# Mixer steps queued behind projections, SSD decays and RG-LRU convolutions one step ahead, FFN residual added on VectorE

## The chip, the cores and the metric

One Trainium2 chip, of which the program uses one core: TensorE (PE, with its weight loads PEld), VectorE (DVE), ScalarE (ACT), GpSimd (POOL) and the queue of SyncE (SP), which issues nearly all transfers. The metric is the device time of one execution in microseconds (us), the median over runs.

## The reference

Two layers of a diffusion backbone on 256 context and 512 latent tokens of width 1024, all float32. Each layer modulates its input, multiplies it by one wide matrix, runs four bidirectional sequence mixers on the parts of the product (A: HGRN2, B: Mamba-2 SSD, C: RG-LRU, D: retention), projects back, and then does the same with a convolutional FFN.

```python
for l in range(DEPTH):
    sh1, sc1, g1, sh2, sc2, g2 = adaln(c, ada_w[l], ada_b[l])
    u = concat([h_ctx * (1 + csc1) + csh1, h_lat * (1 + sc1) + sh1])
    mix = hybrid_mixer(u, w_in[l], ...)          # A, B, C, D, then @ w_out
    h_lat = layer_norm(ALPHA * h_lat + g1 * mix[:, CTX_LEN:], ...)
    f_lat = conv_ffn(h_lat * (1 + sc2) + sh2, ...)   # (gelu(dwconv(gate)) * up) @ w_out
    h_lat = layer_norm(ALPHA * h_lat + g2 * f_lat, ...)
    # the context stream goes the same way, in layer 0 only

def hybrid_mixer(h, ...):
    # B: y = (q k^T * masked exp(b_t - b_s)) v per chunk, plus q S exp(b_t); S carried from chunk to chunk
    # C: cx = conv4(c_x); r, gi = sigmoid(cx @ wa), sigmoid(cx @ wi) per block
    #    h = scan of a = exp(-8 r softplus(-lambda)) with input sqrt(1 - a^2) * gi * cx
    return concat([out_a, out_b, out_c, out_d]) @ w_out
```

## The kernel before, in words

Every matrix product is made of three matmuls: an operand is split into a high part (`A.copy` to fp32r, L289) and a low part (the difference, on DVE, L290), and low·high, high·low and high·high are summed in PSUM. Weights arrive as 128x1088 raw tiles ("wr", on SP's queue) and become pairs "wh", "wl" from a pool of WSP = 9. There are three PSUM slots named "pp" for projections and five ("pm") for everything else. SBUF work tiles of 128x774 come from a pool "t3" of 27 slots, and small ones of 128x256 from "s1" of 6; a tile's request waits until the last reader of the slot's former content is done.

In time, the program is: the adaLN of layer 0 and its modulated input u (0 to about 80 us); layer 0's **interleave** (to about 755); its out passes and last pass (to 912); FFN 0 with its last pass (to 1506); layer 1's interleave (1510 to 2110), out passes (to 2225), FFN 1 (2235 to 2607) and the end.

`interleave` (L1361) walks a list of projections (PROJ) and one of mixers (MIX: C0 C1 A0 A1 BC B0 B1 D0 D1). Each entry is a generator whose `yield` tells how much time its step is thought to take; whichever list lags in that time emits its next step. In projections a step is one PSUM tile: 24 matmuls by `proj_T` (L315, features by tokens) or `proj_N` (L338, tokens by features) and the evacuation. Beside the projections a side stream is drawn: in layer 0 the adaLN columns of blocks 2 to 4, whose matmuls (L433, "ada") read raw weights "wr" straight from the transfer. The emitted instructions are then ordered per engine by a scheduler, which may move an instruction past others on its engine unless a `with after(x)` holds it behind x, or `with HP()` favours it.

The mixers that the change touches: `mixC_gates` (L1139) loads gate weights (gw), convolves a tile of 128 features (L967), splits it, and makes the gates (L1157 on PE, L1159 sigmoids on ACT), then tanh, exp and square root; `mixC_tile` (L1178) makes the scan from them on DVE (L1186 on). `mixB_group` goes over chunks of 128 tokens: it fetches a row of cumulated log decays (the transfer aB<-rowsd, L1071), makes the decay matrix on DVE, POOL and ACT (L1074 to L1078), the score (qkB, L1080, PE), the weights wB (L1087 and L1088 on DVE, L1090 on POOL), and the output (yB, L1093, PE; yiB, L1101, PE), summed on DVE (L1106).

In an FFN, `out_pass` (L1264) adds products of blocks of the hidden features into the rows S2 (on DVE, L1273). Then `gate_residual` multiplies S2 by the gate (POOL, L1281), fetches the residual (hr<-hres, L1283, SP) and adds it (POOL, L1286), and `last_pass` (L1308) does the last block: its evacuation multiplies by the gate (DVE, L1320), adds (POOL, L1321) and gathers the statistics of the layer norm (L1324). The layer norm's own gain and bias rows (bc<-ln_g, ln_b) are fetched by SP (L1244) and scaled on DVE (L1246). `adaln_rows` (L391) makes the remaining adaLN columns beside FFN 0: for each of ten blocks of 1024 columns, eight transfers of weights, and for each of them a multiply (L400) or multiply-add (L403) on DVE into `adac`, followed by a few matmuls (L411).

Of the kernel before, what the change touches and what calls it, by code (L numbers as in the profile page):

```python
# [34 lines left out]
WSP = 9  # L35
# [4 lines left out]
SLOTS = dict(t3=27, s1=6, ss=16, pm=5)  # L40
# [145 lines left out]
def hybrid_backbone_kernel(ctx: ExitStack, tc: tile.TileContext, I: dict, out: bass.AP, plan):  # L186
# [69 lines left out]
    adac = [con.tile([128, 1024], F32, name=f"adac{r}") for r in range(2)]  # L256
# [133 lines left out]
    def adaln_rows(l, blks, conds):  # L390


        for blk in blks:
            for k in range(8):
                raw = wrp.tile([128, 2 * WQ], F32, tag="wr", name="wr")
                SY.dma_start(out=raw[:, :1024], in_=I["ada_w"][l, k * 128:(k + 1) * 128, blk * 1024:blk * 1024 + 1024])
                with HP():
                    for r in conds:
                        if k == 0:
                            V.tensor_scalar(out=adac[r], in0=raw[:, :1024], scalar1=condT[:, k, r:r + 1],  # L400
                                            scalar2=None, op0=MULT)
                        else:
                            V.scalar_tensor_tensor(out=adac[r], in0=raw[:, :1024], scalar=condT[:, k, r:r + 1],  # L403
                                                   in1=adac[r], op0=MULT, op1=ADD)
# [626 lines left out]
    def mixB_group(l, g, stB, pB, prm, xT, y):  # L1031
# [35 lines left out]
        for c in (range(6) if l == 0 else range(2, 6)):  # L1067
# [22 lines left out]
            G.tensor_tensor(out=w, in0=w, in1=a[0], op=MULT)  # L1090
            yp = pm("yB")
# [47 lines left out]
    def mixC_gates(l, ct, st, prm, last):  # L1139
# [8 lines left out]
        yield 2.0  # L1148
# [127 lines left out]
    def gate_residual(S, c, gcols, res_src, alpha):  # L1276

        r = 1 if c < 2 else 0
        for j, lo, hi in pieces(0, 1024):
# [6 lines left out]
            G.tensor_tensor(out=o, in0=o, in1=hr, op=ADD)  # L1286
# [74 lines left out]
    def interleave(proj, streams, side, side_from):  # L1361
# [3 lines left out]
        done, tp = {}, 0.0  # L1365
        tm = [0.0] * len(streams)
        cur, mcur = None, [None] * len(streams)
        while proj or cur or any(streams) or any(mcur):
# [10 lines left out]
            if i is not None and (cur is None or tm[i] <= tp):  # L1379
                step = next(mcur[i][1], None)  # L1380
# [80 lines left out]
    for l in range(DEPTH):  # L1461
# [290 lines left out]
        for c in toks:  # L1752
            gate_residual(S2, c, g2cols, lambda c: hres[c * 128:(c + 1) * 128, :], 1.0)
# [50 lines left out]
```

## Time and profile before

| | us |
|---|---|
| median of 3 runs (lowest, highest) | 2624.53 (2621.78, 2625.5) |
| the profiled execution, its time | 2623.2 |
| the profiled execution, span of its profile | 2621.2 |
| PE busy | 2452.0 (94%) |
| DVE busy | 1669.5 (64%) |
| ACT busy | 1073.3 (41%) |
| POOL busy | 838.4 (32%) |

The mean granted clock of TensorE over the span is 0.974 of full speed. PE is busy nearly throughout, so what is to be read are the places where it isn't, and the places where its clock is down: the page's slices show where, the windows how much, the waits on PE what for.

### The profile page before, as it was taken

To read this page: it belongs to the slowest core of one execution; us is meant where nothing else is said; L and a number is where in the kernel's file an instruction comes from. 1 tells how busy PE (TensorE), PEld (TensorE's weight loads), DVE (VectorE), ACT (ScalarE), POOL (GpSimd) and SP (SyncE) were. 2 spreads that over 40 slices of the span, in tenths; PEclk is the share of its full clock that TensorE was granted. 3 is DMA by queue.
4 is the path that set the end of the run, shared out by engine and by line. 5 is a ranking of instruction groups with operands and counts; after the bars stand their busy time and mean duration, and the time that the engine had idled before them with its cause. 6 is when DMAs were issued, how large, how long until landed. Compare 5 with 4: busy or idle time off the path is not lost.

```text
span 2621.2 us, 40928 instructions
## 1 busy us (share of the span) xinstructions
PE 2452.0 (94%) x15542; PEld 2149.7 (82%) x15542; DVE 1669.5 (64%) x3345; ACT 1073.3 (41%) x2033; POOL 838.4 (32%) x1014
## 2 busy tenths in 40 slices
PE   6989999989999999999999899799988989999997
PEld 3977998888997788878888699688787978888886
DVE  4665656788647877655446557856678757644456
ACT  3883444523232334322323278535442432543331
POOL 0245324255332660000000644533337426400006
PEclk9989999999999999999999899799998999999999
DMA  7136121332264244343324322122132273333333
GB/s 265 57 100 202 57 79 56 110 95 71 83 225 162 82 132 147 114 130 114 120 91 147 112 90 81 59 61 77 51 110 78 78 234 122 113 97 97 97 103 115
DMA packets 200436, 289.15 MB, mean 110 GB/s; under 512 B 15440, under 2 KB 144304, under 8 KB 200240
## 3 DMA queue, kind: packets, MB, share of 16 engines
q1 hardware_dynamic: 200240, 286.53, 34.9%
q8 instruction: 123, 2.02, 0.3%
q14 instruction: 73, 0.60, 0.1%
HBM read 255.94 MB, written 30.54 MB: 109 GB/s over the span
## 4 chain that ended last, share of the span: by engine, by line
PE 58%; DVE 17%; DMA 6%; ACT 4%; POOL 3%; issue 3%; SPq 0%; DVEq 0%; POOLq 0%; ACTq 0%
PE pp L315 31%; PE pp L1264 11%; PE pp L338 8%; DVE wl L290 3%; DMA wr<-ada_w_dram 3%; PE pp L1308 2%; PE sc__pm L669 1%; DMA aB__t<-rowsd 1%; DVE adac L403 1%; DVE cva__t L967 1%; DVE wB__t L1087 1%; DVE tot__t L709 1%; DVE wB__t L1088 1%; PE yD__pm L935 1%; POOL S__t L1286 1%
## 5 line engine op out<-in xcount | busy, mean ns | idle before, releaser
L315 PE MATMUL pp<-uh,wl 128*128 128x512 f32 (+2 forms) x1952 | 674.6, 346 | 10.4 <-DVE gt__t L1713 4.2
L315 PE MATMUL pp<-ul,wh 128*128 128x512 f32 (+2 forms) x1952 | 672.3, 345 | 4.6 <-DVE ul L556 4.6
L315 PE MATMUL pp<-uh,wh 128*128 128x512 f32 (+2 forms) x1952 | 670.1, 343 | 0.0
L289 ACT CAST wh<-wr 128x512 fp32r<-128x512 f32 (+1 forms) x552 | 335.4, 620 | 510.5 <-PE pp L1264 200.9
L290 DVE TENSOR_TENSOR wl<-wr,wh 128x512 fp32r<-128x512 f32 (+1 forms) x552 | 425.3, 788 | 165.6 <-ACT wh L289 164.8
L315 PEld LDWEIGHTS pp<-uh,wl 128*128 128x128 f32 x1952 | 370.6, 190 | 54.4 <-DVE gt__t L1713 5.9
L315 PEld LDWEIGHTS pp<-ul,wh 128*128 128x128 f32 x1952 | 371.1, 190 | 41.4 <-DVE ul L556 5.2
L315 PEld LDWEIGHTS pp<-uh,wh 128*128 128x128 f32 x1952 | 371.1, 190 | 38.4 <-issue 0.8
L338 PE MATMUL pp<-wh,ul 128*128 128x256 f32 (+1 forms) x1216 | 363.0, 298 | 14.7 <-DVE gst__t L1485 12.3
L338 PE MATMUL pp<-wl,uh 128*128 128x256 f32 (+1 forms) x1216 | 356.1, 293 | 0.0
L338 PE MATMUL pp<-wh,uh 128*128 128x256 f32 (+1 forms) x1216 | 355.0, 292 | 0.0
L338 PEld LDWEIGHTS pp<-wh,ul 128*128 128x128 f32 x1216 | 238.1, 196 | 21.4 <-DVE gst__t L1485 14.0
L338 PEld LDWEIGHTS pp<-wh,uh 128*128 128x128 f32 x1216 | 238.0, 196 | 2.3 <-issue 1.2
L338 PEld LDWEIGHTS pp<-wl,uh 128*128 128x128 f32 x1216 | 237.9, 196 | 2.2 <-issue 0.8
L951 POOL MEMSET padF__t<- 128x1 f32 x44 | 4.4, 99 | 632.3 <-DVE gt__t L967 280.7
L1264 PE MATMUL pp<-wh,ccl__t 128*128 128x512 f32 x440 | 174.3, 396 | 0.6 <-DVE ccl__t L1355 0.6
L1264 PE MATMUL pp<-wh,cch__t 128*128 128x512 f32 x440 | 173.5, 394 | 0.0
L1264 PE MATMUL pp<-wl,cch__t 128*128 128x512 f32 x440 | 173.4, 394 | 0.0
L1273 DVE TENSOR_TENSOR S__t<-pp,S__t 128x384 f32<-128x384 f32 (+1 forms) x240 | 89.4, 416 | 75.2 <-PE pp L1264 74.9
L403 DVE SCALAR_TENSOR_TENSOR adac<-wr,condT,adac 128x1024 f32<-128x1024 f32 x70 | 92.2, 1339 | 59.3 <-DMA wr<-ada_w_dram 59.3
L703 POOL TENSOR_TENSOR k__t<-k__t,tot__t 128x384 f32<-128x384 f32 x96 | 101.0, 1065 | 80.8 <-ACT kl__t L655 41.8
L967 DVE SCALAR_TENSOR_TENSOR cva__t<-padF__t,PT,cva__t 128x769 f32<-128x769 f32 (+1 forms) x44 | 40.5, 920 | 101.6 <-ACT cva__t L963 101.4
(346 smaller groups left out, 4398.0 us busy)
## 6 DMA issues: line engine op xcount, KB each, us to landing
wr<-w_in_dram SPq DMA_DIRECT2D x112, 512.0 KB, 3.8
wr<-ffn_w_in_dram SPq DMA_DIRECT2D x88, 512.0 KB, 3.6
wr<-ada_w_dram SPq DMA_DIRECT2D x80, 512.0 KB, 3.9
wr<-ffn_w_out_dram SPq DMA_DIRECT2D x44, 512.0 KB, 4.2
wr<-w_out_dram SPq DMA_DIRECT2D x32, 512.0 KB, 4.9
aB__t<-rowsd SPq DMA_DIRECT2D x40, 256.0 KB, 3.2
adw__t<-ada_w_dram SPq DMA_DIRECT2D x32, 256.0 KB, 5.3
hres<-aff__t SPq DMA_DIRECT2D x28, 192.0 KB, 1.9
```

Of the source, the lines that this page charges most:

```text
L289: A.copy(hi[:, :m], rq)
L290: V.tensor_tensor(out=lo[:, :m], in0=rq, in1=hi[:, :m].bitcast(F32), op=SUB)
L315: PE.matmul(ps[:, :t1 - t0], a[:, cs], b[k // 4][:, k % 4, t0:t1], start=n == 0, stop=n == 23)
L338: PE.matmul(ps[:, :nn], a[k // 4][:, k % 4, ts], b, start=n == 0, stop=n == 23)
L403: V.scalar_tensor_tensor(out=adac[r], in0=raw[:, :1024], scalar=condT[:, k, r:r + 1], in1=adac[r], op0=MULT, op1=ADD)
L669: PE.matmul(sc[64 * hs:64 * hs + 64, j * 64:(j + 1) * 64], kl, ql, start=True, stop=True)
L703: G.tensor_tensor(out=strided(K[p], 0, [[2 * m, nk], [PW + m, 2], [1, m]]), in0=strided(K[p], 0, [[2 * m, nk], [PW + m, 2], [1, m]]), in1= ...
L709: V.tensor_tensor(out=strided(tn, noff, [[nk, 2], [1, nk]]), in0=strided(t, off, [[step, 2], [2, nk]]), in1=strided(t, off + 1, [[step, 2] ...
L967: V.scalar_tensor_tensor(out=o[:, lo:hi], in0=pad[:, lo + j:hi + j], scalar=w(j), in1=acc[:, lo:hi], op0=MULT, op1=ADD)
L1264: PE.matmul(ps, a[:, ts], b, start=n == 0, stop=n == 3 * kt - 1)
L1273: V.tensor_tensor(out=o, in0=src, in1=o, op=ADD)
L1308: PE.matmul(ps, a[:, ts], b, start=n == 0, stop=n == 3 * kt - 1)
```

## The change

It has six parts.

1. `interleave` remembers the last matmul of a projection (`front["proj"]`, set in `proj_T` and `proj_N`) and emits every mixer step under `after` of it: the step's instructions on PE stand behind all matmuls of the projections emitted so far.
2. `mixB_group` makes chunk c's decays, score and weights in a function `weights(c)`, called one chunk ahead of their use, and yields 4.0 once more per group.
3. `mixC_prep` (gate weights, convolution, split) is taken out of `mixC_gates`, and `mC` calls it one tile ahead; its yield goes from 2.0 to 4.0.
4. `adac` is no longer two constant tiles of 128x1024 but four t3 tiles of 128x512: 80 instructions on DVE (10 of L400, 70 of L403) become 160 of half the size.
5. WSP goes from 9 to 8, t3 from 27 to 31 slots, s1 from 6 to 5.
6. `gate_residual` takes the engine of its add as an argument, and in the FFNs it is VectorE: 30 adds (18 in layer 0, 12 in layer 1) go from POOL to DVE.

```diff
-WSP = 9
+WSP = 8
-SLOTS = dict(t3=27, s1=6, ss=16, pm=5)
+SLOTS = dict(t3=31, s1=5, ss=16, pm=5)
...
-                        PE.matmul(ps[:, :t1 - t0], a[:, cs], b[k // 4][:, k % 4, t0:t1],
-                                  start=n == 0, stop=n == 23)
+                        front["proj"] = PE.matmul(ps[:, :t1 - t0], a[:, cs], b[k // 4][:, k % 4, t0:t1],
+                                                  start=n == 0, stop=n == 23)
...
-                            V.scalar_tensor_tensor(out=adac[r], in0=raw[:, :1024], scalar=condT[:, k, r:r + 1],
-                                                   in1=adac[r], op0=MULT, op1=ADD)
+                        for j in range(2):
+                            o, rj = adac[r][j], raw[:, j * 512:j * 512 + 512]
...
+                                V.scalar_tensor_tensor(out=o, in0=rj, scalar=condT[:, k, r:r + 1], in1=o,
+                                                       op0=MULT, op1=ADD)
...
-        for c in (range(6) if l == 0 else range(2, 6)):
+        def weights(c):
...
+            return w
+
+        chs = list(range(6) if l == 0 else range(2, 6))
+        ws = {chs[0]: weights(chs[0])}
+        yield 4.0
+        for c in chs:
+            s = slice(c * 128, (c + 1) * 128)
+            if c + 1 in chs:
+
+                ws[c + 1] = weights(c + 1)
+            w = ws.pop(c)
...
-    def mixC_gates(l, ct, st, prm, last):
+    def mixC_prep(l, ct, st, prm):
...
-        yield 2.0
+        st["c", ct] = (gh, gl, cx, ch, cl)
+        yield 4.0
+
+    def mixC_gates(l, ct, st, prm, last):
+        gh, gl, cx, ch, cl = st.pop(("c", ct))
...
-    def gate_residual(S, c, gcols, res_src, alpha):
+    def gate_residual(S, c, gcols, res_src, alpha, eng=G):
...
-            G.tensor_tensor(out=o, in0=o, in1=hr, op=ADD)
+            eng.tensor_tensor(out=o, in0=o, in1=hr, op=ADD)
...
-                step = next(mcur[i][1], None)
+                with after(front.get("proj")):
+                    step = next(mcur[i][1], None)
...
             for i in range(2):
-                X["lastC"] = yield from mixC_gates(l, 2 * j + i, X["C", j], P, X.get("lastC"))
-                if j or i:
-                    yield from mixC_tile(l, 2 * j + i - 1, X["C", (2 * j + i - 1) // 2], P)
+                yield from mixC_prep(l, 2 * j + i, X["C", j], P)
+                if i:
+                    X["lastC"] = yield from mixC_gates(l, 2 * j, X["C", j], P, X.get("lastC"))
+                if i and j:
+                    yield from mixC_tile(l, 1, X["C", 0], P)
+            X["lastC"] = yield from mixC_gates(l, 2 * j + 1, X["C", j], P, X.get("lastC"))
+            yield from mixC_tile(l, 2 * j, X["C", j], P)
...
-            gate_residual(S2, c, g2cols, lambda c: hres[c * 128:(c + 1) * 128, :], 1.0)
+            gate_residual(S2, c, g2cols, lambda c: hres[c * 128:(c + 1) * 128, :], 1.0, V)
```

The scheduler's order moves with it in many places; three follow. PE has as many instructions as before (14098), DVE 3457 after 3347, ACT 2037 after 2035 (two more table loads), POOL 989 after 1019, SP 821 as before. In the order after, L315 is L314, L338 is L337, L433 is L434, L1273 is L1290, L1286 is L1303, L1320 is L1337, L1246 is L1263.

**DVE at the end of FFN 0.** Before, the last evacuations of the out pass (L1273), four splits of weights, then at once the scaling of the layer norm's rows (L1246) and, behind it, the first evacuations of the last pass (L1320):

```order
L1273 TENSOR_TENSOR S__t_11080<-pp,S__t_11080 128x256
L1273 TENSOR_TENSOR S__t_11137<-pp,S__t_11137 128x256
L290 TENSOR_TENSOR wl<-wr,wh 128x512 x2
L1246 TENSOR_SCALAR bc__t_14626<-bc__t_14626 128x768
L1320 TENSOR_TENSOR gtmp__t_14676<-pp,bc__t_14541 128x384
L1320 TENSOR_TENSOR gtmp__t_14680<-pp,bc__t_14544 128x128
L1246 TENSOR_SCALAR bc__t_14630<-bc__t_14630 128x768
```

Now the residual adds (L1303) stand among and behind the evacuations, the last seven in a row (five of them here), and two evacuations of the last pass (L1337) stand ahead of the first scaling (L1263):

```order
L1303 TENSOR_TENSOR S__t_11082<-S__t_11082,hr__t_14685 128x384
L1303 TENSOR_TENSOR S__t_11084<-S__t_11084,hr__t_14689 128x384
L1303 TENSOR_TENSOR S__t_11161<-S__t_11161,hr__t_14693 128x256
L1303 TENSOR_TENSOR S__t_11104<-S__t_11104,hr__t_14713 128x384
L1303 TENSOR_TENSOR S__t_11161<-S__t_11161,hr__t_14717 128x256
L1337 TENSOR_TENSOR gtmp__t_14774<-pp,bc__t_14639 128x384
L1337 TENSOR_TENSOR gtmp__t_14778<-pp,bc__t_14642 128x128
L1263 TENSOR_SCALAR bc__t_14724<-bc__t_14724 128x768
```

The adds have come in ahead of the last pass's first evacuation, and the scaling has gone behind it.

**PE in layer 0's interleave, the side stream's matmuls "ada".** Before, eight and four of them with five projection matmuls between:

```order
L433 MATMUL ada__pm_1594<-wr,condT 32x256 x8
L315 MATMUL pp<-uh_170,wl 128x384
L315 MATMUL pp<-ul_172,wh 128x384
L315 MATMUL pp<-uh_170,wh 128x384
L315 MATMUL pp<-uh_170,wl 128x384
L315 MATMUL pp<-ul_172,wh 128x384
L433 MATMUL ada__pm_1594<-wr,condT 32x256 x4
```

Now four at a time, the next four 35 matmuls later:

```order
L434 MATMUL ada__pm_1548<-wr,condT 32x256 x4
L314 MATMUL pp<-uh_167,wh 128x384
L314 MATMUL pp<-uh_167,wl 128x384
L314 MATMUL pp<-ul_169,wh 128x384
L314 MATMUL pp<-uh_167,wh 128x384
L314 MATMUL pp<-uh_167,wl 128x384
L314 MATMUL pp<-ul_169,wh 128x384
L314 MATMUL pp<-uh_167,wh 128x384
L314 MATMUL pp<-uh_168,wl 128x384
L314 MATMUL pp<-ul_170,wh 128x384
L1174 MATMUL cgp__pm_1561<-cxl__t_1209,gwh__t_1196 128x384
```

Before, the groups were twelve, eight, eight and four; after a first twelve they now come four at a time, 13 to 36 rows apart but for one pair, with gate matmuls of mixer C (cgp) among them.

**PE in layer 0's mixer B, first group.** Before, the score of a chunk (qkB) stands beside the output of the chunk ahead (yB); the first two scores stand 51 and 32 rows ahead of their own outputs:

```order
L1080 MATMUL qkB__pm_5665<-cvo__t_5170,cvo__t_5098 128x128
L1093 MATMUL yB__pm_5614<-xn__t_5318,wB__t_5604 128x64 x4
L338 MATMUL pp<-wh,ul_172 128x256
L338 MATMUL pp<-wl,uh_170 128x256
L338 MATMUL pp<-wh,uh_170 128x256
L1080 MATMUL qkB__pm_5759<-cvo__t_5170,cvo__t_5098 128x128
```

Now the first two scores stand among the state steps (dlB), 65 and 78 rows ahead of their outputs:

```order
L1059 MATMUL dlB__pm_5492<-vw__s_5490,Bn__t_5318 128x256
L1082 MATMUL qkB__pm_5597<-cvo__t_5168,cvo__t_5096 128x128
L1059 MATMUL dlB__pm_5499<-vw__s_5497,Bn__t_5318 128x256
L1082 MATMUL qkB__pm_5650<-cvo__t_5168,cvo__t_5096 128x128
L1059 MATMUL dlB__pm_5506<-vw__s_5504,Bn__t_5318 128x256
L337 MATMUL pp<-wh,ul_169 128x256
```

The scores have moved up to the state steps, so the weights made from them start earlier; the outputs (yB) come later.

## Rows read from the trace of the kernel before

**Rows 1.** The page: busy time by engine.
```profile
PE 2452.0 (94%) x15542; PEld 2149.7 (82%) x15542; DVE 1669.5 (64%) x3345; ACT 1073.3 (41%) x2033; POOL 838.4 (32%) x1014
```

**Rows 2.** Windows of the span: busy us and count by engine, clock, DMA.
```profile
core 0: us, PE busy (x) PEld busy (x) DVE busy (x) ACT busy (x) POOL busy (x), PEclk, DMA share, GB/s
95.00:230.00 135.00, 116.36 (x817) 106.07 (x816) 88.00 (x115) 98.01 (x156) 61.58 (x36) 0.90 0.39 120
480.00:680.00 200.00, 183.34 (x1378) 174.41 (x1377) 156.72 (x361) 61.55 (x138) 98.55 (x113) 0.97 0.31 94
1200.00:1400.00 200.00, 199.43 (x1064) 168.35 (x1063) 103.48 (x172) 53.73 (x90) 1.32 (x24) 1.00 0.38 119
1450.00:1475.00 25.00, 15.39 (x67) 12.06 (x65) 6.22 (x10) 2.49 (x4) 22.82 (x26) 0.88 0.65 198
1550.00:1700.00 150.00, 128.15 (x830) 122.63 (x829) 104.93 (x135) 115.00 (x185) 67.55 (x42) 0.91 0.22 68
1650.00:1675.00 25.00, 16.09 (x119) 15.11 (x118) 24.56 (x34) 18.41 (x31) 12.82 (x10) 0.79 0.23 74
1895.00:2070.00 175.00, 156.78 (x1178) 148.38 (x1178) 137.76 (x336) 61.30 (x136) 84.75 (x99) 0.94 0.26 81
```

**Rows 3.** Timeline of PE, end of FFN 0: start, length, work, idle before it.
```profile
1476.79 0.77 PE L1308 MATMUL pp<-wh,ccl__t 128*128 128x512 f32 x1 [11.39 <-DVE gtmp__t L1320]
```

**Rows 4.** Timeline of DVE, end of FFN 0.
```profile
1475.07 0.91 DVE L1246 TENSOR_SCALAR bc__t<-bc__t 128x768 f32<-128x768 f32 x1 [14.75 <-DMA bc__t<-ln_b_dram]
```

**Rows 5.** Timeline of SP's queue, end of FFN 0.
```profile
1459.57 9.55 SPq L1283 DMA_DIRECT2D hr__t<-hres  x10
```

**Rows 6.** Timeline of POOL, end of FFN 0.
```profile
1463.54 12.02 POOL L1286 TENSOR_TENSOR S__t<-S__t,hr__t 128x384 f32<-128x384 f32 x14
```

**Rows 7.** Waits of PE, 95:230: us in total, times, longest.
```profile
PE ada__pm L433 <- DMA wr<-ada_w_dram: 14.0, 4, 4.6
```

**Rows 8.** Timeline of PE, 101:108.
```profile
101.49 0.69 PE L1157 MATMUL cgp__pm<-cxl__t,gwh__t 128*128 128x384 f32 x1 [3.22 <-ACT cg__t L1159]
...
105.22 0.43 PE L338 MATMUL pp<-wh,uh 128*128 128x272 f32 x1
105.45 0.43 PE L338 MATMUL pp<-wh,ul 128*128 128x272 f32 x1
...
107.36 0.29 PE L338 MATMUL pp<-wh,ul 128*128 128x272 f32 x1
107.49 0.28 PE L338 MATMUL pp<-wl,uh 128*128 128x272 f32 x1
```

**Rows 9.** Waits of PE, 1550:1700.
```profile
PE pp L338 <- DVE gst__t L1485: 10.4, 4, 5.5
```

**Rows 10.** Waits of DVE in mixer B, 480:680 (layer 0).
```profile
DVE aB__t L1074 <- DMA aB__t<-rowsd: 18.3, 8, 4.7
```

**Rows 11.** Waits of DVE in mixer B, 1895:2070 (layer 1).
```profile
DVE aB__t L1074 <- DMA aB__t<-rowsd: 10.9, 4, 7.4
...
DVE SB__t L1065 <- PE dlB__pm L1058: 3.8, 2, 2.2
```

**Rows 12.** DVE's groups in 915:1440: busy us, mean ns, idle before.
```profile
L403 DVE SCALAR_TENSOR_TENSOR adac<-wr,condT,adac 128x1024 f32<-128x1024 f32 x70 | 92.2, 1339 | 59.3 <-DMA wr<-ada_w_dram 59.3
...
L1273 DVE TENSOR_TENSOR S__t<-pp,S__t 128x256 f32<-128x256 f32 x36 | 13.4, 417 | 7.0 <-PE pp L1264 7.0
L1273 DVE TENSOR_TENSOR S__t<-pp,S__t 128x384 f32<-128x384 f32 x23 | 12.7, 553 | 9.5 <-PE pp L1264 9.5
```

**Rows 13.** DVE's splits of weights in 1200:1400.
```profile
L290 DVE TENSOR_TENSOR wl<-wr,wh 128x512 fp32r<-128x512 f32 x45 | 30.2, 688 | 13.6 <-ACT wh L289 13.5
```

**Rows 14.** DVE's splits of weights in 1455:1480.
```profile
L290 DVE TENSOR_TENSOR wl<-wr,wh 128x512 fp32r<-128x512 f32 x4 | 4.1, 1048 | 0.6 <-ACT wh L289 0.6
```

**Rows 15.** The page: transfers by tile, median us from issue to landing.
```profile
wr<-ada_w_dram SPq DMA_DIRECT2D x80, 512.0 KB, 3.9
```

**Rows 16.** ACT's table loads, one group of them.
```profile
L1173 ACT ACT_TABLE_LOAD x10 | 12.8, 1283 | 0.2
```

More of the change, by code (lines that the diff above doesn't have):

```diff
@@ L255, in hybrid_backbone_kernel @@
     V.tensor_tensor(out=condT[:, :, 0:2], in0=cth, in1=craw, op=MULT)
-    adac = [con.tile([128, 1024], F32, name=f"adac{r}") for r in range(2)]
     sel = con.tile([128, 2, 32], F32, name="sel")
@@ L337, in proj_N @@
                 for a, b in ((ul, w.h(k)), (uh, w.l(k)), (uh, w.h(k))):
-                    PE.matmul(ps[:, :nn], a[k // 4][:, k % 4, ts], b, start=n == 0, stop=n == 23)
+                    front["proj"] = PE.matmul(ps[:, :nn], a[k // 4][:, k % 4, ts], b, start=n == 0, stop=n == 23)
                     n += 1
@@ L393, in adaln_rows @@
         for blk in blks:
+            adac = [[t3("adac")[:, :512] for j in range(2)] for r in conds]
             for k in range(8):
@@ L398, in adaln_rows @@
                     for r in conds:
[L399 to L402, printed above, removed]
-                            V.scalar_tensor_tensor(out=adac[r], in0=raw[:, :1024], scalar=condT[:, k, r:r + 1],
-                                                   in1=adac[r], op0=MULT, op1=ADD)
+                        for j in range(2):
+                            o, rj = adac[r][j], raw[:, j * 512:j * 512 + 512]
+                            if k == 0:
+                                V.tensor_scalar(out=o, in0=rj, scalar1=condT[:, k, r:r + 1], scalar2=None, op0=MULT)
+                            else:
+                                V.scalar_tensor_tensor(out=o, in0=rj, scalar=condT[:, k, r:r + 1], in1=o,
+                                                       op0=MULT, op1=ADD)
                 yield
@@ L410, in adaln_rows @@
                 for j in range(4):
-                    PE.matmul(ps[32 * j:32 * j + 32, :256], sel[:, r, :], adac[r][:, j * 256:(j + 1) * 256],
+                    PE.matmul(ps[32 * j:32 * j + 32, :256], sel[:, r, :], adac[r][j // 2][:, j % 2 * 256:j % 2 * 256 + 256],
                               start=x == 0, stop=x == len(conds) - 1)
@@ L1365, in interleave @@
         done, tp = {}, 0.0
+        front.pop("proj", None)
         tm = [0.0] * len(streams)
```

## The prediction

> **What bounds the kernel now.** Begin with the page's busy times [rows 1]: PE works 2452.0 of 2621.2 us, so at most 169.2 us of idle time can be won, and beside it what TensorE loses where its clock is down (the mean granted clock is 0.974, which over the span is up to 68 us). No other engine is busy for more than 64%. So the chain of PE is the bound, and the question is where it breaks. Next, the windows [rows 2]: in the middle of FFN 0 (1200 to 1400) PE is busy for 199.43 of 200 us at full clock, and nothing is to be had there. The breaks lie in five places, and the change touches all of them.
>
> (a) *The end of FFN 0.* One wait of 11.39 us [rows 3]. The last pass waits for a PSUM slot, that is for an evacuation (L1320) on DVE. DVE has nothing to do for 14.75 us, but the scaling of the layer norm's rows (L1246) stands at its head and waits for their transfer [rows 4]. That transfer stands on SP behind ten loads of residuals, issued over 9.55 us [rows 5], each when a t3 slot comes free, while POOL works off 14 residual adds in 12.02 us [rows 6]. So POOL's adds end the wait, through two queues.
>
> (b) *The side stream in layer 0.* In 95 to 230 PE is idle for 135 - 116.36 = 18.6 us and its clock is 0.90 [rows 2]; 14.0 of it, in four waits, is "ada" matmuls waiting for raw weights [rows 7]. What a wait does to the clock stands in the timeline: after an idle time of 3.22 us at 101.49 the matmuls of 272 columns start 0.23 us apart (105.22, 105.45), from about 107 on 0.13 us apart (107.36, 107.49) [rows 8]. The slow spacing is nearly twice the fast, the lower of the two clock levels, 1.2 and 2.4 GHz. Some 5.7 us at it lose (1 - 0.13/0.23) x 5.7 = 2.5 us, an estimate that I use for each longer wait below.
>
> (c) *From C to A in layer 1* (1550 to 1700): idle 150 - 128.15 = 21.9 us, clock 0.91, so up to 13.5 us more [rows 2]. The largest item is projection matmuls waiting for PSUM slots because DVE evacuates late, 10.4 us [rows 9]; in 1650 to 1675 DVE is busy for 24.56 of 25 us [rows 2].
>
> (d) *Mixer B, both layers*: idle 16.7 us (480 to 680) and 18.2 us (1895 to 2070), clock 0.97 and 0.94, thus another 6 and 10.5 us [rows 2]. DVE meanwhile waits 18.3 and 10.9 us for the decay rows aB [rows 10, 11].
>
> **The change, part by part.** The sum is against the profiled execution's 2623.2 us, 1.3 us below the median of the runs, which I add at the end.
>
> *Residual add on DVE* (a). In the new order DVE has seven adds in a row, then two evacuations of the last pass, and only then the scaling. Nothing on the trace shows this add on DVE; its nearest rows are L1273, the same shapes with one operand in PSUM: 0.553 us for 384 columns, 0.417 us for 256 [rows 12]. The seven are four of 384 and three of 256: 3.5 us. POOL, rid of its adds, has finished its multiplies before 1463.5, where only adds were left [rows 6]; the slots come free, and SP reaches the layer norm's rows some microseconds earlier. If the adds end by about 1467, the first evacuation comes within 2 us of PE's need at 1465.4 (1476.79 - 11.39). Saved: 11.4 + 2.5 for the clock - 1 left = 13 us. Bounds: 2 (the wait only changes its name) and 14 us.
>
> Here a row speaks against the move. A split of weights on DVE, two operands in SBUF, takes 0.688 us in 1200 to 1400, where POOL is busy for 1.32 of 200 us, and 1.048 us in 1455 to 1480, where POOL hardly rests [rows 2, 13, 14]. So an add beside a POOL multiply costs half as much again: 5.3 us for the seven, within the bounds. The Trainium skill, SBUF — State Buffer, "Who interferes with whom", goes further: a VectorE instruction with two SBUF inputs and a GpSimd instruction that reads SBUF exclude each other, and the loser blocks for the whole instruction. By it each of the seven could wait for one whole multiply and the saving would be about 7 us rather than 13, and the median forecast 2590.5 rather than 2584.5. By that rule the trace agrees in kind, but the rows show an increase of a half, no more, and my sum goes by them.
>
> The other 23 adds cost DVE 23 x 0.5 = 12 us. They lie in the out passes, beside matmuls that keep three PSUM slots (each evacuation after some microseconds of matmuls), so at nothing; without that cover, 12.
>
> *Side stream* (b). The order puts groups of four "ada" matmuls 13 to 36 matmuls apart. A raw tile lands 3.9 us after its issue [rows 15]; 24 matmuls of 384 columns take about 24 x 0.18 = 4.3 us (0.18 is 0.13 x 384/272, from rows 8), so most tiles land in time. What moved them is the slower pace of mixer and projection steps, whose yields grew. Of 14.0 us of waits I take 10 away, and 2 us of clock: 12. Bounds 4 and 22 (all waits and four clock dips less 2 us).
>
> *Mixer steps behind projections, C's convolution ahead* (c). PE's in-order queue no longer holds a projection matmul behind a gate or score that isn't ready. But DVE's work stays, and DVE is full at the worst place, so only what is bad order can go: about a third of 21.9 + 13.5, that is 11 us. Bounds: 20, and -4, as DVE's order may get worse for the evacuations.
>
> *Decays a chunk ahead* (d). The aB wait (29.2 us on DVE over both layers) should mostly go, since the transfer is asked for a chunk earlier; but DVE's idle time is not PE's. Of 34.9 idle and 16.5 clock I take a fifth, 10 us. Bounds: 25 and -6.
>
> *Costs.* The halved adac instructions: 1.339 us for 1024 columns [rows 12]; two halves at a split's 0.688 [rows 13] are 1.38. 80 x 0.04 = 3 us of DVE beside FFN 0's matmuls, which wait for nothing: zero; uncovered, 3. Two table loads on ACT at 1.283 us [rows 16], 2.6. One weight slot fewer and one small tile fewer: the weights are ready a unit ahead, so zero, but a single wait would cost about 3.9 us as in rows 15, so 3 for both. In all 6; bounds 0 and 14.
>
> Sum: 2623.2 - 13 - 12 - 11 - 10 + 6 = 2583.2, as a median 2584.5.
>
> **The rivals.** *DVE keeps the mixers.* The waits in (c) and (d) are DVE's capacity (24.56 of 25 us), not order. For it: the change takes no work from DVE, it adds some 18 us. Then only (a) and half of (b) remain: 2624.5 - 13 - 6 + 6 = 2613.5. Against it: DVE waits 29 us for aB, and in 1550 to 1700 is busy for only 104.93 of 150 us. Chance 0.20.
>
> *The waits only change their names.* The adds wait on DVE for multiplies and loads as they did on POOL, the "ada" matmuls for other tiles, and (c), (d) as above: 2624.5 - 2 - 4 + 6 = 2624.5. Chance 0.08; it needs all of it at once.
>
> *Mixers too late.* Each step of a mixer now stands behind up to a whole projection tile, 24 x 0.12 = 2.9 us (256 columns at the pace of rows 8). Mixer B's state steps form a chain, PE to DVE to PE; DVE already waits for PE's part of it, 3.8 us [rows 11]. Ten links in layer 0 and eight in layer 1 make 18 x 2.9 = 52 us. It decides once the projections run out before the chain is done: out pass B waits for B1. Against it: the orders before and after hold nearly as many PE rows behind the last projection tile of layer 1's interleave. With 30 of the 52 us uncovered and 14 won elsewhere: 2640. Chance 0.10.
>
> **How the numbers follow.** My forecast, 2584.5, has a chance of 0.62, and alone a range of 2560 to 2608 (each unknown half-way to its bounds). For 8 in 10 the range reaches down to 2554, where (c) and (d) give near their bounds, and up to 2618, past the first rival. A difference of about 0.2%, 5 us, is what a measurement can tell from none. Faster: 0.62 + nearly all of 0.20 = 0.80; same: 0.08 and a little of the first rival, 0.10; slower: 0.10.
>
> **What would show it.** Right: the 11.39 us wait is gone and PE's granted clock stays 1.0 near 1460 to 1490; "ada" waits under 4 us; aB missing from DVE's waits in B; windows (c) and (d) each several microseconds shorter. Wrong: DVE waiting for POOL or for hr ahead of L1320; projection tiles waiting for L1485 as long as before; PE idle after the last projection of an interleave; weights (L290) among PE's waits, which would be the lost slot.

## The result and the profile after

The changed kernel takes 2590.74 us (median of 4 runs, 2587.09 to 2593.05); the kernel before, in the same comparison, 2625.02 us. The ratio is 0.9868, with a 95% interval of 0.9855 to 0.9881: 34.3 us faster. The forecast was 2584.5, with a range of 2554 to 2618, so its sign, its size and its range held. The sum behind it did not: the profile after and the experiments show that its terms were wrong in both directions.

The page of the changed kernel, busy time by engine, as in [rows 1]:

```profile
span 2585.3 us, 41100 instructions
...
PE 2443.2 (95%) x15542; PEld 2143.5 (83%) x15542; DVE 1697.4 (66%) x3455; ACT 1074.9 (42%) x2035; POOL 820.5 (32%) x984
```

PE's idle time fell from 169.2 to 142.1 us, so 27 of the span's 35.9 us are idle time that went. The other 9 are busy time of the same matmuls; the mean granted clock rose from 0.974 to 0.979, so fewer of them ran at the lower clock. To see where, take three instructions that do the same thing in both kernels: the first projection of FFN 0, the first of layer 1, and the first transposes ahead of FFN 1. The timeline of PE in the kernel before:

```profile
912.27 0.38 PE L315 MATMUL pp<-ul,wh 128*128 128x256 f32 x1 [2.42 <-DVE ul L556]
...
1510.73 0.39 PE L315 MATMUL pp<-ul,wh 128*128 128x256 f32 x1 [1.44 <-DVE ul L556]
...
2226.52 0.53 PE L544 MATMUL ut__pm<-base,S__t 128*128 128x128 f32 x3
```

and in the changed kernel:

```profile
906.67 0.39 PE L314 MATMUL pp<-ul,wh 128*128 128x256 f32 x1 [2.42 <-DVE ul L557]
...
1490.67 0.39 PE L314 MATMUL pp<-ul,wh 128*128 128x256 f32 x1 [2.40 <-DVE ul L557]
...
2189.75 0.78 PE L545 MATMUL ut__pm<-base,S__t 128*128 128x128 f32 x3
```

| stretch | before | after | difference |
|---|---|---|---|
| up to FFN 0 | 912.3 | 906.7 | -5.6 |
| FFN 0 with its last pass | 598.5 | 584.0 | -14.5 |
| layer 1's mixers and out passes | 715.8 | 699.1 | -16.7 |
| FFN 1 and the end | 394.7 | 395.6 | +0.9 |

The windows after, shifted to the same places of the program, beside [rows 2]:

```profile
core 0: us, PE busy (x) PEld busy (x) DVE busy (x) ACT busy (x) POOL busy (x), PEclk, DMA share, GB/s
95.00:230.00 135.00, 118.58 (x873) 106.68 (x872) 101.07 (x123) 97.78 (x159) 65.32 (x38) 0.95 0.37 121
475.00:674.00 199.00, 186.19 (x1432) 179.26 (x1431) 152.10 (x379) 63.05 (x141) 104.14 (x114) 0.97 0.31 94
1434.00:1490.00 56.00, 51.61 (x237) 41.03 (x235) 46.70 (x114) 17.46 (x31) 34.02 (x50) 1.00 0.39 108
1530.00:1680.00 150.00, 132.38 (x868) 127.01 (x867) 105.31 (x130) 116.17 (x186) 64.19 (x36) 0.93 0.23 70
...
1874.00:2046.00 172.00, 156.87 (x1188) 149.17 (x1187) 140.04 (x343) 64.87 (x145) 87.30 (x100) 0.94 0.28 86
```

Each troubled place got a little better, none became clean: idle time in the side stream's window 16.4 us (18.6 before), in mixer B of layer 0 12.8 (16.7), from C to A 17.6 (21.9), in mixer B of layer 1 15.1 (18.2). But a window doesn't hold the same work in both kernels, as the order changed. What an interleave gained as a whole is seen at the last matmul of mixer D, the last mixer in the list; the view gives the first and last start of these matmuls, in layer 0 and in layer 1, in the kernel before:

```profile
L935 PE MATMUL yD__pm<-SD__t,qiD__t x80: 275/275/275, 669.8 to 743.1; 128*128 128x128 f32 x80
...
L935 PE MATMUL yD__pm<-SD__t,qiD__t x64: 275/275/275, 2058.9 to 2118.9; 128*128 128x128 f32 x64
```

and in the changed kernel:

```profile
L936 PE MATMUL yD__pm<-SD__t,qiD__t x80: 275/275/275, 663.8 to 734.1; 128*128 128x128 f32 x80
...
L936 PE MATMUL yD__pm<-SD__t,qiD__t x64: 275/275/275, 2034.9 to 2092.0; 128*128 128x128 f32 x64
```

Layer 0's interleave is 9.0 us shorter, of which its out passes lose 3.4 again (the stretch up to FFN 0 gains 5.6). Layer 1's, counted from its first projection, went from 608.2 to 601.3 us, and its out passes gained the other 10.

The end of FFN 0, timelines of DVE and SP in the changed kernel, beside [rows 4] and [rows 5]:

```profile
1451.19 1.10 DVE L1303 TENSOR_TENSOR S__t<-S__t,hr__t 128x384 f32<-128x384 f32 x1
1452.21 0.68 DVE L289 TENSOR_TENSOR wl<-wr,wh 128x512 fp32r<-128x512 f32 x1
1452.82 2.96 DVE L1303 TENSOR_TENSOR S__t<-S__t,hr__t 128x384 f32<-128x384 f32 x7
1455.69 0.74 DVE L1337 TENSOR_TENSOR gtmp__t<-pp,bc__t 128x384 f32<-128x384 f32 x2
1458.75 0.56 DVE L1263 TENSOR_SCALAR bc__t<-bc__t 128x768 f32<-128x768 f32 x1 [2.31 <-DMA bc__t<-ln_b_dram]
```

```profile
1436.82 11.51 SPq L1300 DMA_DIRECT2D hr__t<-hres  x10
...
1449.09 0.97 SPq L1300 DMA_DIRECT2D hr__t<-hres  x2
1452.32 0.33 SPq L1261 DMA_DIRECT2D bc__t<-ln_g_dram  x1
```

The seven adds in a row take 2.96 us, the evacuations follow at once, and the scaling's wait has shrunk from 14.75 to 2.31 us, behind them. PE's longest wait there (11.39 us before, [rows 3]) is 1.05 us:

```profile
1456.58 0.47 PE L1325 MATMUL pp<-wh,ccl__t 128*128 128x512 f32 x1 [1.05 <-DVE gtmp__t L1337]
```

### The profile page after: what moved, and what is told of

The parts are those of the page before. It is cut to its first block, busy times and chain, and to the rows that moved or that the text cites. A ratio compares the mean times of both kernels' runs of the same rounds, so it can differ in the third digit from the quotient of the medians.

```text
span 2585.3 us, 41100 instructions
## 1 busy us (share of the span) xinstructions
PE 2443.2 (95%) x15542; PEld 2143.5 (83%) x15542; DVE 1697.4 (66%) x3455; ACT 1074.9 (42%) x2035; POOL 820.5 (32%) x984
## 4 chain that ended last, share of the span: by engine, by line
PE 60%; DVE 16%; DMA 6%; ACT 3%; issue 3%; POOL 2%; SPq 0%; DVEq 0%; POOLq 0%; ACTq 0%
PE pp L314 29%; PE pp L1281 14%; PE pp L337 8%; DMA wr<-ada_w_dram 3%; DVE wl L289 3%; DVE adac__t L404 2%; PE pp L1325 2%; PE sc__pm L670 1%; DVE cva__t L968 1%; PE yD__pm L936 1%; DMA aB__t<-rowsd 1%; PE dlB__pm L1059 1%; PE yA__pm L764 1%; PE dlD__pm L899 1%; DVE wB__t L1089 1%
## 5 line engine op out<-in xcount | busy, mean ns | idle before, releaser
L314 PE MATMUL pp<-uh,wl 128*128 128x512 f32 (+2 forms) x1952 | 674.2, 346 | 5.6 <-DVE gt__t L1737 2.8
L314 PE MATMUL pp<-ul,wh 128*128 128x512 f32 (+2 forms) x1952 | 668.4, 343 | 5.5 <-DVE ul L557 5.5
L314 PE MATMUL pp<-uh,wh 128*128 128x512 f32 (+2 forms) x1952 | 672.0, 344 | 0.0
L288 ACT CAST wh<-wr 128x512 fp32r<-128x512 f32 (+1 forms) x552 | 337.9, 621 | 462.1 <-PE pp L1281 230.2
L314 PEld LDWEIGHTS pp<-uh,wl 128*128 128x128 f32 x1952 | 370.8, 190 | 46.3 <-issue 5.0
L314 PEld LDWEIGHTS pp<-ul,wh 128*128 128x128 f32 x1952 | 371.4, 190 | 42.9 <-DVE ul L557 6.5
L314 PEld LDWEIGHTS pp<-uh,wh 128*128 128x128 f32 x1952 | 371.2, 190 | 39.3 <-issue 1.6
L337 PE MATMUL pp<-wh,ul 128*128 128x256 f32 (+1 forms) x1216 | 360.0, 296 | 14.7 <-DVE gst__t L1504 10.5
L337 PE MATMUL pp<-wl,uh 128*128 128x256 f32 (+1 forms) x1216 | 355.5, 292 | 0.0
L337 PE MATMUL pp<-wh,uh 128*128 128x256 f32 (+1 forms) x1216 | 355.3, 292 | 0.0
L337 PEld LDWEIGHTS pp<-wh,ul 128*128 128x128 f32 x1216 | 236.1, 194 | 20.9 <-DVE gst__t L1504 11.8
L337 PEld LDWEIGHTS pp<-wl,uh 128*128 128x128 f32 x1216 | 235.7, 194 | 2.7 <-issue 0.8
L337 PEld LDWEIGHTS pp<-wh,uh 128*128 128x128 f32 x1216 | 235.2, 193 | 2.2 <-issue 0.8
L404 DVE SCALAR_TENSOR_TENSOR adac__t<-wr,condT,adac__t 128x512 f32<-128x512 f32 x140 | 99.7, 763 | 80.3 <-DMA wr<-ada_w_dram 80.2
L1290 DVE TENSOR_TENSOR S__t<-pp,S__t 128x384 f32<-128x384 f32 (+1 forms) x240 | 89.5, 418 | 86.2 <-PE pp L1281 85.9
L1281 PEld LDWEIGHTS pp<-wh,ccl__t 128*128 128x128 f32 x440 | 82.6, 188 | 23.5 <-DVE gt__t L1737 2.5
```

Source lines behind the costliest of these rows:

```text
L288: A.copy(hi[:, :m], rq)
L314: front["proj"] = PE.matmul(ps[:, :t1 - t0], a[:, cs], b[k // 4][:, k % 4, t0:t1], start=n == 0, stop=n == 23)
L337: front["proj"] = PE.matmul(ps[:, :nn], a[k // 4][:, k % 4, ts], b, start=n == 0, stop=n == 23)
L404: V.scalar_tensor_tensor(out=o, in0=rj, scalar=condT[:, k, r:r + 1], in1=o, op0=MULT, op1=ADD)
L1281: PE.matmul(ps, a[:, ts], b, start=n == 0, stop=n == 3 * kt - 1)
L1290: V.tensor_tensor(out=o, in0=src, in1=o, op=ADD)
```

## The experiments

Twelve kernels, each timed in five rounds beside the kernel before, whose median was 2623.8 to 2624.2 us in these. First each part alone or undone, then the slots by number, then two candidates.

### Part 6 alone, and undone

```diff
-            gate_residual(S2, c, g2cols, lambda c: hres[c * 128:(c + 1) * 128, :], 1.0)
+            gate_residual(S2, c, g2cols, lambda c: hres[c * 128:(c + 1) * 128, :], 1.0, V)
```

> The kernel before with part 6 alone: the FFN residual add on VectorE. Theory: POOL's adds made the 11.39 us wait at the end of FFN 0, so it goes or falls under 2 us whatever else is changed, and the time falls by 9 to 13 us, to 2612 to 2616. Rival: the wait went because t3 has 31 slots instead of 27, so that the residual loads no longer hold the layer norm's rows up on SP; then more than 6 us of the wait stays here and the time is 2619 or more.

2617.46 us, ratio 0.9982 (0.9973 to 0.9991): 7 us faster by the medians, 5 by the ratio, less than the 9 to 13 expected. PE's waits in 1440 to 1500:

```profile
PE pp L1308 <- DVE gtmp__t L1320: 4.9, 1, 4.9
```

The wait fell by 6.5 us and a rest stayed: neither theory alone.

```diff
-            gate_residual(S2, c, g2cols, lambda c: hres[c * 128:(c + 1) * 128, :], 1.0, V)
+            gate_residual(S2, c, g2cols, lambda c: hres[c * 128:(c + 1) * 128, :], 1.0)
```

> The changed kernel with part 6 undone: the FFN residual add back on POOL. Theory: the wait of about 11 us at the end of FFN 0 comes back and the time rises by 9 to 13 us, to 2600 to 2604. Rival: 31 slots let the residual loads go early, POOL's adds run beside the out pass, and the time is within 4 us of the changed kernel's 2590.7.

2595.57 us, ratio 0.9898 (0.9883 to 0.9913): slower than the changed kernel by 5 us in the medians, by 8 in the ratios, with PE's wait at 3.7 us:

```profile
PE pp L1325 <- DVE gtmp__t L1337: 3.7, 1, 3.7
```

### Parts 4 and 5 alone: the pools

The kernel before with the new `adaln_rows` and

```diff
-WSP = 9
+WSP = 8
-SLOTS = dict(t3=27, s1=6, ss=16, pm=5)
+SLOTS = dict(t3=31, s1=5, ss=16, pm=5)
```

> The kernel before with parts 4 and 5 alone: adac as four half tiles of t3, WSP 8, t3 31, s1 5. Theory: these parts cost nothing and give the wait of 8.91 us on catT in layer 1's last pass (the spilled tiles are fetched late for want of a t3 slot), so that wait falls under 3 us and the time by 8 to 10 us, to 2615 to 2617. Rival: the catT wait went because the mixers end earlier (parts 1 to 3); then it stays here above 6 us and the time is within 4 us of 2625, or above it if the lost weight slot costs.

2601.91 us, ratio 0.9919 (0.9905 to 0.9932): 22 us faster, two thirds of the whole gain, from the parts that the prediction had booked as costs. The wait at the end of FFN 0 is 4.4 us though the adds are still POOL's:

```profile
PE pp L1309 <- DVE gtmp__t L1321: 4.4, 1, 4.4
```

So that one wait has two causes, and four kernels make a table of it: 11.4 us (27 slots, POOL), 4.9 (27, DVE), 4.4 (31, POOL), 1.05 (31, DVE; this is the changed kernel, with parts 1 to 3, which with the adds on POOL has 3.7).

The second longest wait of PE, that of the transposes catT in layer 1's out passes, went from 8.91 us to 4.28. Before, it was

```profile
2155.35 0.48 PE L1612 MATMUL catT__pm<-base,cy__t 128*128 128x128 f32 x1 [8.91 <-DVE catl L1355]
```

Here the slots can be seen at work. In the kernel before, SP's timeline has the last two fetches of spilled outputs of mixer B behind those of the layer norm's rows,

```profile
2147.23 0.42 SPq L1244 DMA_DIRECT2D bc__t<-ln_b_dram  x1
2147.71 0.42 SPq L1587 DMA_DIRECT2D cy__t<-ysp1B  x1
...
2148.70 0.38 SPq L1587 DMA_DIRECT2D cy__t<-ysp1B  x1
```

and DVE stands idle for 11.22 us until the first of them land:

```profile
2151.27 0.43 DVE L1246 TENSOR_SCALAR bc__t<-bc__t 128x512 f32<-128x512 f32 x1 [11.22 <-DMA cy__t<-ysp1B]
```

The instruction at its head is the scaling of the layer norm's rows (L1246), the same that held the last pass up at the end of FFN 0 [rows 4]. It works on the rows fetched at 2147.23, so the spilled output that the profile names need not be what it waited for; all were asked for late together, when a multiply on POOL (L1589, 2146.09 to 2146.82) had ended. With 31 slots the spilled outputs are issued 40 us earlier, while the program is only 10 us ahead there (mixer D's last matmul at 2108.9 in place of 2118.9):

```profile
2107.73 2.29 SPq L1588 DMA_DIRECT2D cy__t<-ysp1B  x2
```

A loss stands against it in layer 0, a new wait for weights; PE's timeline of the pools alone:

```profile
179.41 0.69 PE L314 MATMUL pp<-uh,wl 128*128 128x384 f32 x1 [9.76 <-DVE wl L289]
```

In part it takes the place of the "ada" waits, which fall from 14.0 us to 6.5 in this kernel.

### Part 1 alone, and undone

```diff
-                step = next(mcur[i][1], None)
+                with after(front.get("proj")):
+                    step = next(mcur[i][1], None)
```

(with `front["proj"]` set in `proj_T` and `proj_N`; undone, the same lines the other way round)

> The kernel before with part 1 alone: each mixer step behind the projection matmuls emitted so far. Theory: of the gains in the mixers, most of that from C to A in layer 1 (5 to 9 us) is from this, and little of that in mixer B: 2616 to 2620, with the waits for ada weights in layer 0 as in the kernel before, since the steps' costs are unchanged. Rival: without the decays and convolutions a step ahead, steps behind a projection tile only come later, and the time is the same or up to 15 us longer: 2624 to 2640.

2627.03 us, ratio 1.0009 (0.9999 to 1.0019): nothing.

> The changed kernel with part 1 undone: mixer steps no longer held behind projections. Part 1 alone gave nothing (2627.0 beside 2624.0). Theory: it gives nothing here either, 2588 to 2594, the stretch from C to A in layer 1 within 3 us of the changed kernel. Rival: it pays only together with the steps made ahead (parts 2 and 3), which else push projections back on PE: then the time rises by 5 us or more, to 2596 or above, with the loss in the mixers of either layer.

2588.5 us, ratio 0.9864 (0.9849 to 0.9878), the changed kernel's within the intervals. Alone, or undone alone, the queueing is worth nothing. The prediction had given it, with part 3, the 11 us from C to A.

### Part 2 undone

`weights(c)` goes back into the loop over chunks, without the extra yield:

```diff
-        ws = {chs[0]: weights(chs[0])}
-        yield 4.0
-        for c in chs:
+        for c in (range(6) if l == 0 else range(2, 6)):
```

> The changed kernel with part 2 undone: mixer B's decays, scores and weights made in their own chunk's step again. Theory: the 3 to 6 us that each layer's mixer B gained come from this, so the time rises by 4 to 9 us, to 2595 to 2600, and VectorE waits 15 us or more for the aB transfers in layer 0 again. Rival: more t3 slots alone let the transfers go early, part 2 adds nothing: 2588 to 2594, with the aB waits under 8 us.

2587.86 us, ratio 0.9865 (0.9846 to 0.9884): nothing. And the decay waits, which part 2 was to remove, don't come back. DVE's waits for them in layer 0 (470 to 680), with part 2 undone, in the changed kernel, and with the pools alone, one row each:

```profile
DVE aB__t L1075 <- DMA aB__t<-rowsd: 7.9, 7, 2.2
```

```profile
DVE aB__t L1076 <- DMA aB__t<-rowsd: 7.8, 7, 2.4
```

```profile
DVE aB__t L1075 <- DMA aB__t<-rowsd: 8.2, 7, 2.3
```

Before, it was 18.3 us [rows 10]. The pools alone take most of that away: the aB tiles are t3 tiles, and with 31 slots a request a chunk earlier adds nothing. That the fetches waited for a slot, and not for their turn on SP, is argued from the kernel's text; with 30 slots the order of steps counts too, as the first of the two candidates shows.

### Part 3 undone

`mixC_prep` goes back into `mixC_gates`, and `mC` to its old order:

```diff
-                yield from mixC_prep(l, 2 * j + i, X["C", j], P)
-                if i:
-                    X["lastC"] = yield from mixC_gates(l, 2 * j, X["C", j], P, X.get("lastC"))
+                X["lastC"] = yield from mixC_gates(l, 2 * j + i, X["C", j], P, X.get("lastC"))
```

> The changed kernel with part 3 undone: mixer C's convolution and split in the same step as its gates again. Theory: the convolution ahead brings little, since gate matmuls wait for ACT's release of PSUM slots (5.15 us at 1616) and not for the convolution: 2589 to 2595. Rival: the gain of about 9 us up to 1724 from C to A is its work: 2597 to 2601, with waits of the gate matmuls for the split (DVE) above 3 us.

2597.23 us, ratio 0.9894 (0.9877 to 0.991): 6.5 us slower than the changed kernel, at the edge of what the rival said, but at another place. The loss is in layer 0, where the wait for weights that the pools alone have comes back:

```profile
178.60 0.69 PE L314 MATMUL pp<-uh,wl 128*128 128x384 f32 x1 [9.78 <-DVE wl L289]
```

The split waits for its cast on ACT, and ACT's timeline there has the cast (L288) behind three table loads and the gates of mixers C and A:

```profile
168.01 1.28 ACT L1181 ACT_TABLE_LOAD   x1
...
170.26 1.28 ACT L618 ACT_TABLE_LOAD   x1
...
173.15 1.28 ACT L1181 ACT_TABLE_LOAD   x1
...
177.21 1.12 ACT L288 CAST wh<-wr 128x512 fp32r<-128x512 f32 x2
```

So part 3 pays by keeping that conflict away. The kernel before has no such wait, nor have those with 28 or 29 t3 slots below; the two that have it are those with eight weight slots, 31 t3 slots and no part 3. The gain is less than the wait, as the "ada" waits, 5.9 us in 95 to 260 with part 3 undone, are 12.7 in the changed kernel.

### The slots by number

Three kernels: the changed one with nine weight slots and 30 t3 slots; the kernel before with adac in t3, 29 slots, weights and small tiles as before; and the kernel before with one weight slot traded for one t3 slot, adac untouched.

```diff
-WSP = 8
+WSP = 9
-SLOTS = dict(t3=31, s1=5, ss=16, pm=5)
+SLOTS = dict(t3=30, s1=5, ss=16, pm=5)
```

> The changed kernel with the ninth weight slot back and 30 t3 slots instead of 31. Theory: the slots gained by moving adac into the pool carry the change, from 27 to about 30; the ninth weight slot is worth 0 to 4 us (with the pools changed alone, a wait of 9.76 us for weights arose at 179) and the 31st t3 slot about as little: 2586 to 2593. Rival: the time hangs on the last t3 slot: 2596 or more.

2589.34 us, ratio 0.9867 (0.9852 to 0.9882): the same. The ninth weight slot and the 31st t3 slot are worth nothing measurable against each other.

```diff
-SLOTS = dict(t3=27, s1=6, ss=16, pm=5)
+SLOTS = dict(t3=29, s1=6, ss=16, pm=5)
```

> The kernel before with adac as four half tiles of t3, t3 29, and the weight and small-tile slots as before (9 and 6): parts 4 and 5 without the lost slots, and with two t3 slots fewer than the pools alone had (31, at 2601.9). Theory: the time falls with the number of t3 slots that are free when adac isn't in use, so two more than before give about half of the 22 us: 2609 to 2617, with the catT wait between 4 and 9 us and no 9.8 us wait for weights at 179. Rival: the two slots suffice and the lost weight slot cost the pools alone some 8 us in layer 0: 2594 to 2602.

2612.44 us, ratio 0.9948 (0.9934 to 0.9961): about half of the pools' gain, as expected.

```diff
-WSP = 9
+WSP = 8
-SLOTS = dict(t3=27, s1=6, ss=16, pm=5)
+SLOTS = dict(t3=28, s1=6, ss=16, pm=5)
```

> The kernel before with a weight slot traded for one t3 slot (WSP 8, t3 28), adac as before. Theory: t3 slots carry the gain, one gives 3 to 8 us: 2616 to 2621. Rival: the gain of the pools alone came from adac's halves and not from slots, and a lost weight slot costs: 2624 or more.

2613.12 us, ratio 0.9957 (0.9945 to 0.9969). One slot more, adac where it was, and 11 us gone: more than the theory gave one slot, but clear of the rival, by which the gain came from adac's halves. With 27, 28, 29 and 31 slots the four kernels take 2624, 2613, 2612 and 2602 us (with 29 and 31, adac takes four of the slots beside FFN 0); the steps are not even. In this last one the wait at the end of FFN 0 is still 10.0 us:

```profile
PE pp L1308 <- DVE gtmp__t L1320: 10.0, 1, 10.0
```

so its gain lies elsewhere; its catT wait is 4.37 us in place of 8.91:

```profile
2147.50 0.47 PE L1612 MATMUL catT__pm<-base,cy__t 128*128 128x128 f32 x1 [4.37 <-DVE catl L1355]
```

### Two candidates

The changed kernel without parts 1 and 2, with WSP 9, t3 30, and

```diff
-            gate_residual(S2, c, g2cols, lambda c: hres[c * 128:(c + 1) * 128, :], 1.0, V)
+            gate_residual(S2, c, g2cols, lambda c: hres[c * 128:(c + 1) * 128, :], 1.0, V if l == 0 else G)
```

> The changed kernel without parts 1 and 2, which gave nothing when undone, with nine weight slots and 30 t3 slots, and the residual add on VectorE in layer 0's FFN only (in layer 1 it goes back to POOL). Theory: the parts that carried the gain are all in it, and the end of FFN 1, where the changed kernel lost 2 us, is as before: 2580 to 2588. Rival: what parts 1 and 2 move is a matter of chance in the order, and the time is within 3 us of the changed kernel's 2590, or above it.

2598.64 us, ratio 0.9892 (0.9878 to 0.9906): 8 us slower than the changed kernel, though each of its pieces undone or altered by itself cost nothing. The parts don't add up, and the traces show where. The kernel with nine weight and 30 t3 slots (2589.34 us) differs from this one by parts 1 and 2 and by the engine of layer 1's adds. In layer 0, which holds only parts 1 and 2 of that, mixer D's last matmul starts at 733.4 us with them and at 743.6 without, and VectorE's waits for the decay rows (480 to 680) are 7.4 us with them and 15.9 without. In this order:

```profile
L936 PE MATMUL yD__pm<-SD__t,qiD__t x80: 275/275/275, 659.7 to 733.4; 128*128 128x128 f32 x80
```

```profile
L936 PE MATMUL yD__pm<-SD__t,qiD__t x80: 275/275/421, 666.2 to 743.6; 128*128 128x128 f32 x80
```

```profile
DVE aB__t L1076 <- DMA aB__t<-rowsd: 7.4, 3, 4.3
```

```profile
DVE aB__t L1075 <- DMA aB__t<-rowsd: 15.9, 7, 4.1
```

So parts 1 and 2, each worth nothing when undone by itself with 31 slots, are together worth some 9 us with 30 (2598.64 beside 2589.34 us; the four runs of this kernel spread from 2590.32 to 2600.31, and the two intervals just touch). Either part may stand in for the other, or the 31st slot for both. No run undoes the two together with 31 slots, or one of them with 30, so which it is stays open.

The last edit alone, on the changed kernel as it is:

> The changed kernel with the residual add on VectorE in layer 0's FFN only; in layer 1 it goes back to POOL. Theory: at the end of FFN 1 the adds on VectorE make the last pass wait for evacuations (two waits of 1.4 us at 2553 and 2557 that the kernel before didn't have); without them the time falls by 1 to 3 us, to 2587 to 2590, and the wait of 1.05 us at the end of FFN 0 stays as it is. Rival: the last pass of FFN 1 waits for VectorE anyway, or the order of the end shifts the loss elsewhere: 2590 or more.

2587.11 us, ratio 0.9857 (0.9837 to 0.9878), against 0.9868 (0.9855 to 0.9881) for the changed kernel: not to be told apart. No version was found that clearly beats it.

## Why the prediction was right, and where its steps failed

**The total** was forecast at -40 us and measured at -34.3. It came out partly by luck: a gain that the sum didn't have took the place of gains that were smaller than forecast.

**Costs, +6 (bounds 0 and 14).** This is the step that failed most. It priced what the pools lost, a weight slot, a small tile, halved instructions, and gave no term to the four t3 slots that they won. Parts 4 and 5 alone give -22 us. The rows to see it by were quoted: [rows 5] were read as loads that wait for a t3 slot, and [rows 10, 11] show transfers that VectorE waits for. These transfers were not slow: an aB fetch of layer 0 lands 3.1 us after its issue before and 3.5 after (medians), while VectorE's waits for them fell to less than half. They were asked for late. The halves cost more than 3 us: 160 instructions took 109.8 us where 80 took 101.0, as DVE's groups of the changed kernel in 907 to 1434 show beside [rows 12], which lack the first of these lines of the kernel before:

```profile
L400 DVE TENSOR_SCALAR adac<-wr,condT 128x1024 f32<-128x1024 f32 x10 | 8.8, 900 | 17.6 <-PE ada__pm L411 16.9 <-DMA wr<-ada_w_dram 0.8
...
L404 DVE SCALAR_TENSOR_TENSOR adac__t<-wr,condT,adac__t 128x512 f32<-128x512 f32 x140 | 99.7, 763 | 80.3 <-DMA wr<-ada_w_dram 80.2
...
L402 DVE TENSOR_SCALAR adac__t<-wr,condT 128x512 f32<-128x512 f32 x20 | 10.1, 543 | 6.4 <-DMA wr<-ada_w_dram 5.8 <-PE pp L1281 0.6
```

That they are hidden held as far as the stretch shows: FFN 0 as a whole is 14.5 us shorter, a little more than (a) was to give.

**(a), -13 (bounds 2 and 14).** The wait went (11.39 to 1.05 us), and the seven adds took 2.96 us, below the 3.5 worked out. But "POOL's adds end the wait" was half of it: part 6 alone is worth 5 to 7 us and, where the slots are there, 5 to 8. The rival of the first run, slots for the residual loads, was the other half. By the rule of the Trainium skill, SBUF — State Buffer, "Who interferes with whom", that the prediction quotes, each of the seven could have waited for a whole multiply, and the saving would have been about 7 us. The seven didn't wait, since POOL's last multiply before them ended at 1451.87 and they began at 1452.82; adds that did meet one are in the last section.

**(b), -12 (bounds 4 and 22).** Failed in its mechanism. The "ada" waits, of which 10 us were to go, hardly fell, from 14.0 [rows 7] to 12.7 us; what came is clock, 0.95 after 0.90 in the window of 135 us, about 7 us where 2 were forecast. PE's waits of the changed kernel in 95 to 260:

```profile
PE ada__pm L434 <- DMA wr<-ada_w_dram: 12.7, 3, 7.7
```

There are fewer (3 for 4) but one of them is longer. The prediction put the wider spacing down to mixer and projection steps whose yields grew; only two yields of mixers did. Wider spacing does not help when the raw tiles are asked for late, and SP's waits in 150 to 215 say that they are: it waits 21.1 us for splits of weights (10.8 before) ahead of "ada" loads (L428):

```profile
SPq L428 <- DVE wl L289: 21.1, 4, 10.4
```

That this is the reason is argued from this row, not tried. Part 3, which the prediction counted under (c), is what keeps this stretch from losing.

**(c), -11, and (d), -10.** About half came, with (b). Layer 1's interleave holds (c) and half of (d), 16 us by the forecast, and gained 6.8; layer 0's holds (b) and the other half, 17 us, and gained 9.0. What was to win it is not shown to have won it: with 31 slots, part 1 or part 2 undone costs nothing, and the pools alone bring the decay waits from 18.3 to 8.2 us. Only with both undone and 30 slots do these waits and some 9 us come back. Two of the signs for being right failed: aB is still among VectorE's waits in B (7.8 and 6.7 us), and the "ada" waits aren't under 4 us. One sign for being wrong came: in window (c) projection tiles wait for their evacuation almost as long as the 10.4 us of [rows 9].

```profile
PE pp L337 <- DVE gst__t L1504: 9.1, 3, 5.2
```

That fits the first rival, by which VectorE's capacity and not the order sets these waits; it wasn't tested by itself. Its time is out by 23 us, and by two in its own sum (2624.5 - 13 - 6 + 6 is 2611.5, not 2613.5). For the decays it named the wrong resource, since more slots shortened those waits.

**Not in the sum at all:** the catT wait in layer 1, 8.91 us before, 1.29 after. It was in the trace, the second longest single wait of PE after the start, and had no term, as no edit was near it. VectorE's queue had the scaling of the layer norm's rows at its head there, the thing that (a) had read at the end of FFN 0.

**The slower rival** did not come: mixer steps behind projections cost nothing, alone (1.0009, 0.9999 to 1.0019) or in the changed kernel (2590.74 us with them, 2588.50 without).

**What stays open.** Which of parts 1 and 2 and the last t3 slot stands in for which was not tried, nor parts 2 and 3 alone on the kernel before. Each edit also makes the scheduler write another order on every engine, and no run holds the order fixed and alters the slots alone: that the slots themselves, and not the orders that came with them, gave the 22 us rests on three kernels with more slots, all faster, and on the waits that fell in them. The time does not go with their number alone.

## What to carry to other kernels

Ask of a wait for a transfer when it was issued, and of a late issue which slot it waited for: here the pool edits alone gave two thirds of the gain of a change whose other parts had the names. Price what a pool wins as carefully as what it loses. And where a scheduler writes the order, test each part alone and undone before crediting it, and undo together those that serve the same wait: a right total can come from wrong terms, and a part that costs nothing when undone may only be covered by another.

## What the runs showed of the hardware

An add of 128x384 on VectorE, both operands in SBUF, took 1.10 us at 1451.19 while POOL multiplied,

```profile
1449.70 2.17 POOL L1298 TENSOR_TENSOR S__t<-S__t,bc__t 128x384 f32<-128x384 f32 x2 [2.57 <-DVE S__t L1290]
```

twice the 0.55 us of L1273 [rows 12], and over all 30 adds from 0.41 to 1.63 us with a median of 0.55:

```profile
L1303 DVE TENSOR_TENSOR S__t<-S__t,hr__t x30: 411/548/1633, 1418.2 to 2557.2; 128x384 f32<-128x384 f32 x20, 128x256 f32<-128x256 f32 x10
```

Set beside POOL's instructions one by one, the 30 fall in two groups in the changed kernel's trace: the 19 that no POOL instruction overlaps took 0.41 to 0.56 us, the 11 that one overlaps 0.95 to 1.63. That a VectorE instruction with two SBUF inputs and a GpSimd instruction that reads SBUF contend, and that the lock between them is exclusive, is what the Trainium skill, SBUF — State Buffer, "Who interferes with whom", states, and these adds bear it out: the longest began 0.07 us after a POOL instruction of 1.29 us and took 1.1 us more than the median. In the prediction the rows' "half as much again" was an average and hid this: the four splits of [rows 14] took from 0.72 to 1.50 us. Halving an instruction of 1.339 us gave two of 0.763 us, 14% more in all.
